# RWKV-7 stage of a bidirectional trunk: sums with the identity and with r, the diagonal blocks and a copy of U moved from VectorE to TensorE and ScalarE

## The chip, the cores and the metric

The kernel runs on one core of one Trainium2 chip. The metric is the device time of one launch in microseconds (us). The core has five engines with instruction streams of their own: TensorE (PE), VectorE (DVE), ScalarE (ACT), GpSimd (POOL) and SyncE (SP), which here issues most of the DMA transfers. TensorE's clock is granted by a throttle at one of two levels, 1.2 or 2.4 GHz; PEclk in the tables is the granted clock as a share of 2.4 GHz, averaged over a stretch.

## The reference

A trunk of two layers over 256 context and 512 latent tokens of width 1024, in fp32. Layer 0 has mLSTM heads beside differential attention, layer 1 has RWKV-7 heads beside gated linear attention, and each layer ends in an MLP. The change lies in the RWKV-7 heads alone: 8 heads of 64 channels, a scan over tokens in both directions (context first, then latents):

```python
def rwkv7_scan(r, decay, k, v, kk, a, state):
    def step(S, inp):
        r_t, w_t, k_t, v_t, kk_t, a_t = inp
        sk = jnp.einsum('bhei,bhi->bhe', S, kk_t)
        S = S * w_t[:, :, None, :] - sk[..., None] * (kk_t * a_t)[:, :, None, :] + v_t[..., None] * k_t[:, :, None, :]
        return S, jnp.einsum('bhei,bhi->bhe', S, r_t)
```

Decay, a and k come from `tanh` and `sigmoid` of small products of the tokens; kk is the unit key. After the scan the outputs are normed per head, a bonus `r . k v` is added, and a gate multiplies them. The kernel's products of this stage run on fp32 operands, for which the trace shows two records each.

## The kernel before

The scan is worked in chunks of 64 tokens. The function `rwkv` (from line 1497) takes the 8 heads as 4 pairs; a pair fills the 128 partitions, head 0 in rows 0 to 63 and head 1 in rows 64 to 127 (`OWN`; `OTH` are the other head's columns). A *unit* is four chunks of a pair in both scan directions (8 chunk matrices): per pair one unit of context and two of latents, so 12 units, u = 0 to 11. Names in a listing of the program number units from 1: `BK_8` and `AT_8` belong to u = 7.

Within a chunk the recurrence is a triangular system. With alpha the decayed unit keys (`ABD`), beta and kappa the scaled keys divided by the decay (`BK`), A = beta . alpha, and U = (I - A)^-1, state and output of a chunk are one product each with [state | values] (`X`): matrices E and F (`EF`), to which an identity (for the state) and the decayed r (`R`, for the output) are added.

`front(u)` makes what does not hang on the state:
- two products with a `tanh` behind each (L1606, tiles `th` and `ta`), +1 (L1612), the scan over the chunk (L1614), exponentials (L1633, L1634);
- `ABD` (L1640), held as a 128x128 matrix per chunk with the two heads as diagonal blocks and zeros elsewhere, in two buffers whose zeros are written once: VectorE writes head 0's blocks, GpSimd head 1's;
- `BK` (L1658 VectorE, L1660 GpSimd), `Rbd` (L1706);
- eight transposes of `ABD` on TensorE, read out by four ScalarE copies into `GT`;
- A: eight products `ABD` x `BK` (tiles `mm<-BK,abd`), read out to `AT` (L1681 ScalarE) and `GT` (L1682 VectorE);
- `DG`, the 16x16 blocks on A's diagonal: for each of four block rows a column of a 0/1 matrix (`sel`) times a slice of `AT`, summed by four VectorE instructions (L1719, L1721);
- `DG` goes by DMA to DRAM (`scrA`, L1723) and comes back with one block per partition (`lnA`, L1727). The blocks are inverted there: 14 small instructions (L1742, L1744), then L1752, a reduction on VectorE (L1754), L1755, a reduction (L1757). GpSimd does it for u from 2 on, VectorE for u = 0 and 1. The inverse goes by DMA to `scrU` (L1758).

`back(u)` fetches it (`UN`, L1766), writes it into the two halves of `U` by two masked copies (L1773), and merges blocks of 16 to 32 and 64 by small products (tiles `mg`), into `UB`.

`chain(u)` walks the four chunks: `ready` prepares `RB` and `Gt`, `solve` computes EF in PSUM and VectorE adds the identity (L1871) and R (L1874) while reading it out, `move` gives the next state (tiles `sy`, scaled into `X` at L1890) and the output (tiles `y`).

A loop over u = 0 to 14 interleaves, step by step, `chain(u-2)`, `back(u-1)`, `front(u)` and, for each pair's end, the norm of the outputs. The instructions so issued are then put in one static order per engine by a scheduler that works with modelled times; on the chip each engine executes its own list in that order and waits by semaphores. The tile `mm` in PSUM has three buffers, taken in the program's order. SP issues the transfers of the inverse in its own order, too.

Of the kernel before, what the change touches and what calls it, by code (L numbers as in the profile page):

```python
# [12 lines left out]
AF = mybir.ActivationFunctionType  # L13
ALU = mybir.AluOpType
AX = mybir.AxisListType
PSUM = bass.MemoryType.PSUM
DRAM = bass.MemoryType.DRAM
# [19 lines left out]
U_EX = 0  # L37
# [22 lines left out]
def shape_constants():  # L60
    """Constants that follow from the shapes alone: identity, block means, masks, rope tables."""
# [29 lines left out]
def shape_masks():  # L91
    """int32 masks: levels of the gated attention within blocks of 64"""
    s = np.arange(P)
    segs = {}
    a, b = s[:, None] % 64, np.arange(64)[None]
    for lv in range(6):
        m = 1 << lv
        same = (a // (2 * m)) == (b // (2 * m))
        segs[f"gf{lv}"] = same & ((a // m) % 2 == 0) & ((b // m) % 2 == 1)
        segs[f"gb{lv}"] = same & ((a // m) % 2 == 1) & ((b // m) % 2 == 0)  # L100
    segs["gd"] = a == b
    return segs
# [10 lines left out]
def layout(a):  # L113
    """tokens as columns (context, then latents); the small parameters as columns of one array"""
# [48 lines left out]
class Paced:  # L163
    """the tensor engine; instructions of side work are issued after the main work that precedes them"""
# [20 lines left out]
def trunk(ctx, tc, xc, pk, ada_w, w_in_even, w_in_odd, w_out, w_mlp_in, w_mlp_out, diff_lam, rwkv_w2, rwkv_a2,  # L185
# [40 lines left out]
    # ---------------------------------------------------------------- constants, parameters  # L226
# [84 lines left out]
    def weave(main, side, every):  # L311
        """runs main; after each `every` steps of it a step of side; then the rest of side"""
# [6 lines left out]
    def logsig(out, z, t):  # L319
        """out = log(sigmoid(z)), stable; t is scratch; out may be z only if z is SBUF"""  # L320
# [5 lines left out]
    def spread(rc, n, psum):  # L326
        """[token, tile, head] columns -> psum tiles [(h, 64), tokens] (4 tiles of 128 tokens each)"""
# [18 lines left out]
    # ---------------------------------------------------------------- adaLN modulation  # L346
# [40 lines left out]
    def norm_gain(l, which):  # L387
        """g * (1 + scale) as [P, 8, 2]"""
# [7 lines left out]
    # ---------------------------------------------------------------- building blocks  # L396
# [4 lines left out]
    def wload(pieces, kt=KT, cols=P, zero=False, rows=None):  # L401
        """pieces: (column, DRAM AP [n*128, m]) -> hi and lo parts [P, kt, cols] of all its row tiles or those in rows"""
# [21 lines left out]
    def mm3(w, at, xs, spans, bank=None):  # L424
        """three passes of one 128-column weight tile; xs: list of (hi, lo) tiles per k; yields psum per span"""
# [14 lines left out]
    def mm3_steps(w, at, xs, spans, res, group=1):  # L440
        """mm3 in steps of `group` row tiles"""
# [15 lines left out]
    def at(x, t0, t1):  # L457
        """tokens t0..t1 of a tile that holds all tokens or the latents only"""
# [31 lines left out]
    def norm_out(xT, l, which, rs, np_, spans=SPANS, first=False):  # L490
        """normed and modulated residual -> hi/lo tiles"""
# [5 lines left out]
        def shifted_parts(k):  # L497
            """adds the shift, splits"""
# [66 lines left out]
    # ---------------------------------------------------------------- scratch of the mLSTM gates  # L565
# [13 lines left out]
    # ---------------------------------------------------------------- load the residual  # L579
# [21 lines left out]
    def put_o(i, src, t0=0, t1=T, keep=None):  # L601
        """o^T tile i (fp32, SBUF) -> hi/lo parts, in DRAM or in the pool that keeps them"""
# [95 lines left out]
            # n = b - m, g = i - b, per tile: state scale exp(g + n_last), carry exp(n_last + m_prev)  # L698
# [126 lines left out]
    def head_out(i, hs, sq, sm, ps_, gain, gate):  # L825
        """rms norm of [tokens, 2 heads, 64] in natural layout, transposed, times gain (and gate) -> o^T tile i"""
# [19 lines left out]
    # ---------------------------------------------------------------- layer 0: differential attention heads  # L846
# [3 lines left out]
    def diff_prep(p, res, fin=None):  # L850
        """projections of a pair of heads, in steps"""
# [32 lines left out]
                # one Newton step on the table's result  # L884
# [65 lines left out]
    def diff_attn(fill, tail_open, tail):  # L950
        with ExitStack() as es:
# [13 lines left out]
            def scores(u):  # L965
                """softmax numerators of a unit's two maps, combined"""
# [47 lines left out]
            def finish(p, u):  # L1014
                """rms norm; the first softmax's sum divides here"""
# [28 lines left out]
            class Side:  # L1044
                """work in steps, done at a rate"""
# [55 lines left out]
    def out_proj(l, xT, oT, spans, ks=tuple(range(KT)), dts=range(KT)):  # L1101
        """adds the gated projection of the mixer tiles ks to the tiles dts of the residual"""
# [23 lines left out]
            # the first tiles' products do not wait for the sums over the residual  # L1126
# [65 lines left out]
    def tail():  # L1192
        """the part of the output projection that does not wait for the last pair of heads"""
# [33 lines left out]
    # ---------------------------------------------------------------- layer 1: gated linear attention heads, and  # L1227
    # the projections of the RWKV-7 heads
# [69 lines left out]
    def gla():  # L1298
# [4 lines left out]
        with ExitStack() as es:  # L1303
# [14 lines left out]
            # in-tile sums of the log decays  # L1318
# [69 lines left out]
                    # states: k decayed to the end of its tile  # L1388
# [640 lines left out]
```

## Time and profile before

| | |
|---|---|
| median of 3 runs | 2432.72 us (2432.2 to 2434.35) |
| span of the profiled execution, first to last instruction (no other time of that execution is given) | 2438.6 us |
| PE, DVE, ACT, POOL busy over the span | 91%, 56%, 38%, 14% |
| RWKV-7 stage, 1640 to 2005 us: PE, DVE, ACT, POOL busy | 284.5, 287.6, 182.3, 170.2 of 365 us |
| granted TensorE clock in that stage, and over the span | 0.83, 0.935 |

Before and behind that stage TensorE is busy with the large projections and the MLP. The stage is the one in which no engine is busy all the time: the table's row says 78% for PE and 79% for DVE. Busy time of PE is the union of its matmuls' times, which overlap at their ends; one record stands for a transpose.

### The profile page before, as it was taken

How to read it: one execution, taken by the hardware profiler on the slowest of the kernel's cores; microseconds unless marked ns; L12 is line 12 of the kernel's file. 1: busy time of each engine (PE TensorE's matmuls, PEld its weight loads, DVE VectorE, ACT ScalarE, POOL GpSimd, SP SyncE). 2: the span in 40 equal slices, each digit the busy share in tenths (PEclk: the TensorE clock that was granted, in tenths of full speed). 3: DMA queues.
4: the chain of work that ended last, by engine and by line, in shares of the span. 5: the costliest groups of instructions: out<-in, count | busy, mean ns of one | idle time of the engine just before them, and what ended most of it. 6: DMA issues, size and time to landing. Idle time of an engine off the chain costs nothing.

```text
span 2438.6 us, 40627 instructions
## 1 busy us (share of the span) xinstructions
PE 2219.0 (91%) x16676; PEld 1857.2 (76%) x16676; DVE 1360.4 (56%) x2616; ACT 929.7 (38%) x1785; POOL 333.5 (14%) x470
## 2 busy tenths in 40 slices
PE   5999888988899999999998999965888789999999
PEld 3888665656788888888886778854767677998997
DVE  4667645645664343343433575768778856544543
ACT  2444444545543122221323633324555543422322
POOL 3110001002100000000003021323546530000000
PEclk7999898989999999999997998976878989999999
DMA  6343468875312222222232212121010143333333
GB/s 236 78 117 103 138 191 250 257 245 169 109 54 60 61 69 62 61 61 61 67 105 58 61 44 76 64 74 23 15 31 12 32 119 91 87 96 89 94 96 95
DMA packets 293739, 232.26 MB, mean 95 GB/s; under 512 B 40705, under 2 KB 265890, under 8 KB 293554
## 3 DMA queue, kind: packets, MB, share of 16 engines
q1 hardware_dynamic: 284434, 188.65, 26.3%
q0 software_dynamic: 9120, 41.03, 5.6%
q8 instruction: 131, 2.15, 0.4%
q14 instruction: 54, 0.44, 0.1%
HBM read 203.06 MB, written 26.58 MB: 94 GB/s over the span
## 4 chain that ended last, share of the span: by engine, by line
PE 72%; DVE 11%; DMA 8%; POOL 3%; ACT 3%; issue 3%; SPq 0%; DVEq 0%; ACTq 0%; POOLq 0%
PE mm L170 60%; PE po L170 3%; PE ps L170 3%; DMA aw<-in_ada_w_dram 2%; PE gps L170 2%; DMA scrU<-lnV 1%; PE pb L170 1%; PE re L170 1%; DMA lnA<-scrA 1%; PE oy L170 1%; DMA scrA<-DG 1%; DMA UN<-scrU 1%; DMA stk<-qd 1%; POOL lnT L1742 1%; POOL lo L512 1%
## 5 line engine op out<-in xcount | busy, mean ns | idle before, releaser
L170 PE MATMUL mm<-hi,wh 128*128 128x512 f32 (+2 forms) x1816 | 495.2, 335 | 5.1 <-DVE uq L649 3.1
L398 ACT ACTIVATE wh<-wr 128x1024 fp32r<-128x1024 f32 (+1 forms) x203 | 213.7, 1052 | 750.0 <-PE mm L170 715.7
L170 PE MATMUL mm<-lo,wh 128*128 128x256 f32 (+2 forms) x1816 | 487.6, 331 | 0.4 <-DVE lo L555 0.4
L170 PE MATMUL mm<-hi,wl 128*128 128x256 f32 (+2 forms) x1816 | 485.9, 331 | 0.3 <-DVE wl L399 0.3
L170 PEld LDWEIGHTS mm<-hi,wh 128*128 128x128 f32 x1816 | 328.6, 192 | 40.5 <-issue 6.0
L170 PEld LDWEIGHTS mm<-lo,wh 128*128 128x128 f32 x1816 | 330.9, 192 | 33.5 <-issue 1.8
L170 PEld LDWEIGHTS mm<-hi,wl 128*128 128x128 f32 x1816 | 330.3, 192 | 33.0 <-issue 1.4
L399 DVE TENSOR_TENSOR wl<-wr,wh 128x1024 fp32r<-128x1024 f32 (+1 forms) x203 | 249.9, 1231 | 96.6 <-ACT wh L398 93.1
L170 PE MATMUL mm<-mhi,wl 128*128 128x512 f32 (+1 forms) x768 | 233.1, 359 | 0.5
L170 PE MATMUL mm<-mhi,wh 128*128 128x512 f32 (+1 forms) x768 | 232.6, 358 | 0.0
L170 PE MATMUL mm<-mlo,wh 128*128 128x512 f32 (+1 forms) x768 | 232.5, 358 | 0.0
L1152 DVE SCALAR_TENSOR_TENSOR xT<-mm,mod,xT 128x256 f32<-128x256 f32 (+1 forms) x96 | 60.6, 659 | 289.6 <-PE mm L170 289.6
L170 PEld LDWEIGHTS mm<-mhi,wl 128*128 128x128 f32 x768 | 144.3, 188 | 25.7 <-DVE wl L399 2.3
L170 PEld LDWEIGHTS mm<-mlo,wh 128*128 128x128 f32 x768 | 144.3, 188 | 23.3
L170 PEld LDWEIGHTS mm<-mhi,wh 128*128 128x128 f32 x768 | 144.1, 188 | 23.1
L512 POOL TENSOR_TENSOR lo<-nh,hi 128x768 fp32r<-128x768 f32 x13 | 28.8, 2240 | 695.8 <-DVE nh L507 654.6
L980 DVE TENSOR_REDUCE mx<-pb 128x1 f32<-128x768 f32 (+1 forms) x96 | 73.5, 775 | 64.8 <-PE pb L170 64.2
L1139 DVE COPY wb<-mm 128x2 f32<-128x2 f32 x64 | 10.2, 159 | 176.1 <-PE mm L170 176.1
L170 PE MATMUL mm<-aw,sv 128*32 128x256 f32 x768 | 64.6, 435 | 31.3 <-DMA aw<-in_ada_w_dram 30.9
L982 ACT ACTIVATE pp<-pb,mx 128x768 f32<-128x768 f32 (+1 forms) x96 | 72.5, 758 | 34.2 <-DVE mx L980 33.2
L399 DVE TENSOR_TENSOR mlo<-mr,mhi 128x768 fp32r<-128x768 f32 (+1 forms) x64 | 52.7, 825 | 48.3 <-ACT mhi L398 48.3
L1001 ACT ACTIVATE wT<-po 128x384 f32<-128x384 f32 (+1 forms) x80 | 37.5, 469 | 101.4 <-PE po L170 101.1
(535 smaller groups left out, 3652.5 us busy)
## 6 DMA issues: line engine op xcount, KB each, us to landing
aw<-in_ada_w_dram SPq DMA_DIRECT2D x96, 512.0 KB, 6.4
wr<-in_w_mlp_in_dram SPq DMA_DIRECT2D x64, 512.0 KB, 4.0
wr<-in_w_mlp_out_dram SPq DMA_DIRECT2D x64, 512.0 KB, 3.6
wr<-in_w_in_even_dram SPq DMA_DIRECT2D x28, 512.0 KB, 8.3
wr<-in_w_in_odd_dram SPq DMA_DIRECT2D x27, 512.0 KB, 3.8
stk<-qd POOLq DMA_DIRECT2D x32, 384.0 KB, 8.2
e<-nd SPq DMA_DIRECT2D x24, 256.0 KB, 4.2
xT<-in_xc_dram SPq DMA_DIRECT2D x8, 384.0 KB, 6.8
```

What stands on the lines that cost most here:

```text
L170: ins = getattr(self.eng, name)(*a, **k).ins
L398: act.activation(out=hi, in_=src, func=AF.Copy)
L399: dve.tensor_tensor(out=lo, in0=src, in1=hi.bitcast(F32), op=ALU.subtract)
L512: (dve if first and k in (0, 3, 6) else pool).tensor_tensor(out=lo[:, a0:a1], in0=h[:, a0:a1], in1=hi[:, a0:a1].bitcast(F32), op=ALU.subtract)
L980: dve.tensor_reduce(out=mx[:, c_:c_ + 1], in_=ps[:, :kk], axis=AX.X, op=ALU.max, negate=True)
L982: act.activation(out=pp[:, :kk], in_=ps[:, :kk], func=AF.Exp, bias=mx[:, c_:c_ + 1], accum_out=l[:, c_:c_ + 1])
L1001: act.activation(out=u["wT"][:, a0 * P:a1 * P], in_=u["po"][:, P:(1 + a1 - a0) * P], func=AF.Copy)
L1139: dve.tensor_copy(out=wb, in_=q[:, 0:nb])
L1152: dve.scalar_tensor_tensor(out=at(xT[dt], t0, t1), in0=q, scalar=mods[l][:, 5, dt, s_:s_ + 1], in1=at(xT[dt], t0, t1), op0=ALU.mult, op1=A ...
L1742: inv.tensor_tensor(out=w_, in0=A8[:, :, j, 0:j].unsqueeze(3).to_broadcast([64, 2, j, n]), in1=V8[:, :, j:j + 1, j:8].to_broadcast([64, 2, ...
```

## The change

Six pieces of `rwkv` change; the line numbers of what follows them shift by three. Comments and docstrings are dropped besides.

1. U is written by ScalarE, both halves (`U_EX`), instead of VectorE.
2. `th` + 1 is a ScalarE activation instead of a VectorE instruction.
3. `ABD` is dense, [channel, direction, chunk, 64], by two VectorE instructions over all 128 partitions; GpSimd has no part in it, and the buffer is one of a pool of two.
4. The eight transposes are 16 products of 64x64 with the identity, head 0 in the upper left quarter of TensorE's array and head 1 in the lower right, into one PSUM bank, read out by one ScalarE copy of 128x512. The products for A are 16 of 64 rows instead of eight of 128. `GT` holds alpha in columns 0 to 63 for both heads, so the copies to `Gt` reverse the halves for head 1.
5. `DG` is the sum of four products with `Dsel`, the columns of `sel` as diagonal matrices (made once), in a PSUM bank of `mm`, and one ScalarE copy.
6. EF is read out by one ScalarE copy; the identity comes in as four more products `id2` x `X` behind the four of `sy`, in the same bank, and R as four more products in `y`.

```diff
-U_EX = 0
+U_EX = 2
...
+            Dsel = tl(kp, [P, 4, P], "Dsel")
+            for e in range(4):
+                dve.tensor_scalar(out=Dsel[:, e], in0=ident, scalar1=C["sel"][:, e:e + 1], scalar2=None, op0=ALU.mult)
...
-                ABD = ABDs[u % 2]
+                ABD = tl(pp_, [P, 2, 4, 64], "abd")
...
-                dve.tensor_scalar(out=th, in0=th, scalar1=1.0, scalar2=None, op0=ALU.add)
+                act.activation(out=th, in_=th, func=AF.Copy, bias=1.0)
...
-                for h in range(2):
-                    q = OWN[h]
-                    for d in range(2):
-                        (pool if (h, d) >= (SPL_A, 0) else dve).tensor_tensor(out=ABD[q, d, :, q], in0=CH(src("kk", d))[q],
-                                                           in1=c4[q, d, :, 0:64], op=ALU.mult)
+                for d in range(2):
+                    dve.tensor_tensor(out=ABD[:, d], in0=CH(src("kk", d)), in1=c4[:, d, :, 0:64], op=ALU.mult)
...
-                for d in range(2):
-                    ps = mm()
-                    for c_ in range(4):
-                        transpose(ps[:, c_ * P:(c_ + 1) * P], ABD[:, d, c_])
-                    p3 = ps.rearrange("p (c t) -> p c t", t=P)
+                ps = mm()
+                for j in range(8):
                     for h in range(2):
-                        (dve.tensor_copy if h < GT_EV else act_copy)(GT[OWN[h], d, :, OWN[h]], p3[OWN[h], :, OWN[h]])
+                        q = OWN[h]
+                        pe.matmul(ps[q, 64 * j:64 * j + 64], ABD[q, j // 4, j % 4], ident[q, q], start=True, stop=True,
+                                  tile_position=(64 * h, 64 * h))
+                act_copy(flat(GT)[:, :, 0:64], CH(ps))
...
-                        pe.matmul(ps[:, c_ * P:(c_ + 1) * P], ABD[:, d, c_], BK[:, d, c_], start=True, stop=True)
+                        for h in range(2):
+                            q = OWN[h]
+                            pe.matmul(ps[q, c_ * P:(c_ + 1) * P], ABD[q, d, c_], BK[q, d, c_], start=True, stop=True,
+                                      tile_position=(64 * h, 64 * h))
...
-                dve.tensor_scalar(out=DG, in0=flat(AT)[:, :, 0:16], scalar1=sel(0), scalar2=None, op0=ALU.mult)
-                for e in range(1, 4):
-                    dve.scalar_tensor_tensor(out=DG, in0=flat(AT)[:, :, 16 * e:16 * e + 16], scalar=sel(e), in1=DG,
-                                             op0=ALU.mult, op1=ALU.add)
+                ps = mm()[:, 0:P]
+                for e in range(4):
+                    pe.matmul(ps.rearrange("p (j t) -> p j t", t=16), Dsel[:, e], flat(AT)[:, :, 16 * e:16 * e + 16],
+                              start=e == 0, stop=e == 3)
+                act_copy(DG.rearrange("p j t -> p (j t)"), ps)
...
-                    if more:
-                        dve.tensor_tensor(out=own(EF), in0=own(ef), op=ALU.add, in1=ident.rearrange(
-                            "p (h c) -> p h c", h=2).unsqueeze(1).to_broadcast([P, 2, 2, 64]))
-                    if lat:
-                        dve.tensor_tensor(out=oth(EF), in0=oth(ef), in1=R[:, :, c_], op=ALU.add)
+                    part = (lambda a: a) if lat and more else own if more else oth
+                    act_copy(part(EF), part(ef))
...
+                        for d in range(2):
+                            for h in range(2):
+                                pe.matmul(ps[OWN[h], 64 * d:64 * d + 64], id2[OWN[h]], X[OWN[h], d, c_, h],
+                                          start=False, stop=d == 1, tile_position=(64 * h, 64 * h))
...
+                        for own_ in range(2):
+                            for d in range(2):
...
+                                    q = OWN[h] if own_ else slice(0, P)
+                                    e = R[q, d, c_, q] if own_ else EF[:, d, 64 + 64 * h:128 + 64 * h]
```

The scheduler orders every engine's list anew. GpSimd's list at the inverse of u = 3 (its tiles end in `_4`), beside the front of u = 4 (`abd0`, `BK_5`, `kd_5`, `Rbd0`), in the kernel before:

```order
L1744 TENSOR_TENSOR lnV_4_14889<-lnV_4_14889,lnT_4_14891 64x2x3x5
L1640 TENSOR_TENSOR abd0_1_13782<-kkl_2_14552,cs_5_15077 64x4x64 x2
L1742 TENSOR_TENSOR lnT_4_14891<-lnA_4_14888,lnV_4_14889 64x24
L1744 TENSOR_TENSOR lnV_4_14889<-lnV_4_14889,lnT_4_14891 64x2x2x6
L1660 TENSOR_TENSOR BK_5_14959<-kd_5_15140,pm__5_15080 64x8x64
L1742 TENSOR_TENSOR lnT_4_14891<-lnA_4_14888,lnV_4_14889 64x14
L1660 TENSOR_TENSOR BK_5_14959<-kd_5_15140,pm__5_15080 64x8x64
L1744 TENSOR_TENSOR lnV_4_14889<-lnV_4_14889,lnT_4_14891 64x2x7
L1706 TENSOR_TENSOR Rbd0_1_13943<-rl_6_14545,cs_5_15077 64x4x64 x2
L1752 TENSOR_TENSOR lnT_4_14891<-lnA_4_14888,lnV_4_14889 64x512
L1755 TENSOR_TENSOR lnT_4_14891<-lnV_4_14889,lnW_4_14937 64x512
```

The same place in the changed kernel:

```order
L1747 TENSOR_TENSOR lnV_4_14971<-lnV_4_14971,lnT_4_14973 64x2x3x5
L1745 TENSOR_TENSOR lnT_4_14973<-lnA_4_14970,lnV_4_14971 64x24
L1747 TENSOR_TENSOR lnV_4_14971<-lnV_4_14971,lnT_4_14973 64x2x2x6
L1745 TENSOR_TENSOR lnT_4_14973<-lnA_4_14970,lnV_4_14971 64x14
L1747 TENSOR_TENSOR lnV_4_14971<-lnV_4_14971,lnT_4_14973 64x2x7
L1755 TENSOR_TENSOR lnT_4_14973<-lnA_4_14970,lnV_4_14971 64x512
L1660 TENSOR_TENSOR BK_5_15056<-kd_5_15243,pm__5_15177 64x8x64 x2
L1709 TENSOR_TENSOR Rbd0_1_13957<-rl_6_14601,cs_5_15174 64x4x64 x2
L1758 TENSOR_TENSOR lnT_4_14973<-lnV_4_14971,lnW_4_15034 64x512
```

`abd` is gone from the list, and `BK` of the next unit stands behind the first of the two large instructions instead of inside the 14 small ones.

TensorE's list around u = 7 (`BK_8`) and the merges of u = 6 (`U_7`), before:

```order
L170 MATMUL mm_402_16352<-BK_8_16119,abd1_1_13783 128x128 x4
L170 MATMUL mm_403_16372<-BK_8_16119,abd1_1_13783 128x128 x4
...
L170 MATMUL mm_405_16485<-twd_1_10820,w2_1_10804 128x256 x2
...
L170 MATMUL mg_25_16136<-U_7_16114,AT_7_15980 32x32 x32
...
L170 MATMUL mg_26_16186<-VT_13_16134,TD_13_16133 32x32 x32
...
L170 MATMUL mg_27_16248<-U_7_16114,AT_7_15980 32x32 x16
```

And in the changed kernel (`Dsel` is the selection of the diagonal blocks, `twd` the first product of u = 8's front):

```order
L170 MATMUL mg_25_16342<-U_7_16319,AT_7_16153 32x32 x32
L170 MATMUL y_7_15895<-Rbd1_1_13958,X_6_15455 64x64 x3
L170 MATMUL mm_402_16598<-BK_8_16324,abd_8_16326 64x128 x8
...
L170 MATMUL mg_27_16453<-U_7_16319,AT_7_16153 32x32 x16
...
L170 MATMUL mm_404_16664<-AT_8_16565,Dsel_1_13784 128x128 x4
...
L170 MATMUL mm_405_16729<-twd_1_10820,w2_1_10804 128x256 x2
```

A's products for the unit, and the selection of its diagonal blocks, stood ahead of the merges of the unit before (the selection on VectorE, behind the read-out of A); half of the products and the selection now stand behind the first, or the first three, steps of those merges. The selection stands behind a merge step of the unit before at eight of the eleven units that follow another (names 2, 3, 4, 6, 7, 8, 10 and 11): at 6 and 8 behind the third step, at 3 partly so, at the others behind the first. From that first step to the selection the list of these eight has 67 rows of other work in all, none at 2 and 15 at 6.

## Rows read from the trace of the kernel before

**Rows 1.** Windows: start:end, us, busy of PE, PEld, DVE, ACT, POOL; clock; DMA share

```profile
1640.00:2005.00 365.00, 284.50 (x4215) 242.47 (x4216) 287.59 (x694) 182.28 (x471) 170.17 (x265) 0.83 0.14 34
2005.00:2440.00 435.00, 426.82 (x2630) 378.43 (x2630) 209.67 (x336) 141.15 (x208) 0.00 (x0) 0.99 0.32 94
```

**Rows 2.** Instructions on tile DG: count, min/median/max ns, first to last start

```profile
L1723 SPq DMA_DIRECT2D scrA<-DG x12: 319/320/432, 1649.7 to 1964.6; - x12
```

**Rows 3.** Timeline of SP: start us, us, instruction; the transfers of DG

```profile
1734.03 0.32 SPq L1723 DMA_DIRECT2D scrA<-DG  x1
...
1761.60 0.43 SPq L1723 DMA_DIRECT2D scrA<-DG  x1
...
1783.57 0.32 SPq L1723 DMA_DIRECT2D scrA<-DG  x1
...
1825.64 0.32 SPq L1723 DMA_DIRECT2D scrA<-DG  x1
```

**Rows 4.** Chain of waits, 1738 to 1765 us, in order of time: start, us

```profile
1743.65 1.51 POOL abd L1640 x2
...
1747.50 1.34 POOL BK L1660
1748.83 0.04 issue
1748.88 2.08 PE mm L170 x8
...
1753.15 0.89 PE mm L170 x8
```

**Rows 5.** Timeline of POOL: start us, us, [idle before]; two inverses

```profile
1707.75 0.21 POOL L1742 TENSOR_TENSOR lnT<-lnA,lnV 64x14 f32<-64x14 f32 x1 [4.47 <-DMA lnA<-scrA]
...
1713.50 2.17 POOL L1752 TENSOR_TENSOR lnT<-lnA,lnV 64x512 f32<-64x512 f32 x1
...
1739.37 0.21 POOL L1742 TENSOR_TENSOR lnT<-lnA,lnV 64x14 f32<-64x14 f32 x1 [3.90 <-DMA lnA<-scrA]
...
1750.60 2.18 POOL L1752 TENSOR_TENSOR lnT<-lnA,lnV 64x512 f32<-64x512 f32 x1
```

**Rows 6.** Timeline of DVE: the reads of U

```profile
1789.47 0.48 DVE L1773 TENSOR_SCALAR U<-UN,cs 128x128 f32<-128x128 f32 x2 [2.24 <-DMA UN<-scrU]
...
1987.00 0.48 DVE L1773 TENSOR_SCALAR U<-UN,cs 128x128 f32<-128x128 f32 x2 [5.98 <-DMA UN<-scrU]
```

**Rows 7.** Timeline of PE, 1987 to 2003 us: merges and a late chunk

```profile
1987.63 1.06 PE L170 MATMUL mg<-U,AT 32*32 32x32 f32 x64 [2.85 <-DVE U L1773]
...
1994.04 0.69 PE L170 MATMUL mg<-U,AT 32*32 32x32 f32 x32
...
2001.41 0.45 PE L170 MATMUL sy<-X,EF 128*64 128x64 f32 x8
2001.69 0.40 PE L170 MATMUL y<-EF,X 128*64 128x64 f32 x8
2002.03 0.71 PE L170 MATMUL re<-RB,Gt 128*128 128x128 f32 x4
```

**Rows 8.** ACT by line and form, stage: busy us, mean ns | idle before

```profile
L1825 ACT ACTIVATE GT<-mm 64x256 f32<-64x256 f32 x48 | 18.2, 378 | 27.8 <-PE mm L170 27.2
L1825 ACT ACTIVATE RB<-re 128x256 f32<-128x256 f32 x43 | 16.4, 382 | 23.3 <-PE re L170 22.2 <-ACT Gt L1825 0.7
...
L1912 ACT ACTIVATE yo<-y 128x512 f32<-128x512 f32 x3 | 1.8, 597 | 0.1
```

**Rows 9.** DVE by line and form, stage: what the change takes away

```profile
L1871 DVE TENSOR_TENSOR EF<-re,cs 128x256 f32<-128x256 f32 x42 | 17.7, 421 | 11.9 <-PE re L170 11.0
...
L1721 DVE SCALAR_TENSOR_TENSOR DG<-AT,cs,DG 128x128 f32<-128x128 f32 x36 | 12.3, 342 | 0.4
L1874 DVE TENSOR_TENSOR EF<-re,Rbd 128x256 f32<-128x256 f32 x29 | 12.0, 414 | 2.1 <-PE re L170 2.0
...
L1612 DVE TENSOR_SCALAR th<-th 128x512 f32<-128x512 f32 x11 | 6.1, 558 | 6.2 <-ACT th L1606 6.2
L1773 DVE TENSOR_SCALAR U<-UN,cs 128x128 f32<-128x128 f32 x24 | 6.1, 297 | 22.0 <-DMA UN<-scrU 22.0
...
L1719 DVE TENSOR_SCALAR DG<-AT,cs 128x128 f32<-128x128 f32 x12 | 4.4, 363 | 0.4
```

More of the change, by code (lines that the diff above doesn't have):

```diff
@@ L1543, in rwkv @@
             dve.memset(CH(rst)[:, :, 0:1], 0.0)
-            ABDs = zeros(tz, [P, 2, 4, P], "abd")
             load_constants(kp, 2)
+            Dsel = tl(kp, [P, 4, P], "Dsel")
+            for e in range(4):
+                dve.tensor_scalar(out=Dsel[:, e], in0=ident, scalar1=C["sel"][:, e:e + 1], scalar2=None, op0=ALU.mult)
             UBs = zeros(kp, [P, 2, 4, P], "UB", 1, dve)
@@ L1681, in front @@
                         act.activation(out=AT[q, d], in_=p3[q, :, q], func=AF.Copy)
-                        dve.tensor_tensor(out=GT[q, d, :, o_], in0=p3[q, :, o_], op=ALU.mult,
+                        dve.tensor_tensor(out=GT[q, d, :, 64:128], in0=p3[q, :, o_], op=ALU.mult,
                                           in1=C["mlt"][q].unsqueeze(1).to_broadcast([64, 4, 64]))
@@ L1716, in front @@
                 sA, sU = scrA[u % 3], scrU[u % 3]
-                sel = lambda n: C["sel"][:, n:n + 1]
                 DG = tl(pp_, [P, 8, 16], "DG")
-                dve.tensor_scalar(out=DG, in0=flat(AT)[:, :, 0:16], scalar1=sel(0), scalar2=None, op0=ALU.mult)
-                for e in range(1, 4):
-                    dve.scalar_tensor_tensor(out=DG, in0=flat(AT)[:, :, 16 * e:16 * e + 16], scalar=sel(e), in1=DG,
-                                             op0=ALU.mult, op1=ALU.add)
+                ps = mm()[:, 0:P]
[3 more added lines that the diff above has]
+                act_copy(DG.rearrange("p j t -> p (j t)"), ps)
                 sp.dma_start(out=sA, in_=DG.rearrange("p j t -> p (j t)"))
@@ L1856, in ready @@
                         pe.matmul(ps[:, d * P:d * P + P], UB[:, d, c_], GT[:, d, c_], start=True, stop=True)
+                    half_ = lambda a: a.rearrange("p d (a c) -> p d a c", a=2)
                     for h in range(2):
-                        (dve.tensor_copy if h < G_EV else act_copy)(Gt[c_ % 2][OWN[h], h], D2(ps[OWN[h], 0:256]))
+                        o_ = half_(Gt[c_ % 2][OWN[h], h])
+                        act_copy(o_[:, :, ::-1] if h else o_, half_(D2(ps[OWN[h], 0:256])))
                     yield
@@ L1884, in move @@
                                 pe.matmul(ps[OWN[h], 64 * d:64 * d + 64], EF[:, d, 192 * h:192 * h + 64], X[:, d, c_, h],
-                                          start=True, stop=True, tile_position=(0, 64 * h))
+                                          start=d == 0, stop=False, tile_position=(0, 64 * h))
+                        for d in range(2):
+                            for h in range(2):
+                                pe.matmul(ps[OWN[h], 64 * d:64 * d + 64], id2[OWN[h]], X[OWN[h], d, c_, h],
+                                          start=False, stop=d == 1, tile_position=(64 * h, 64 * h))
                         sy = ps[:, 0:128].rearrange("p (d c) -> p d c", d=2)
@@ L1892, in move @@
                     if lat:
-                        for d in range(2):
-                            j = 4 * (g - 1) + c_
-                            j = j if d == 0 else 7 - j
-                            for h in range(2):
-                                e = EF[:, d, 64 + 64 * h:128 + 64 * h]
-                                pe.matmul(S["y"][OWN[h], 64 * j:64 * j + 64], X[:, d, c_, h], e if d == 0 else e[:, ::-1],
-                                          start=(g == 1 and c_ == 0 and d == 0), stop=(g == 2 and c_ == 3 and d == 1),
-                                          tile_position=(0, 64 * h))
+                        for own_ in range(2):
+                            for d in range(2):
+                                j = 4 * (g - 1) + c_
+                                j = j if d == 0 else 7 - j
+                                for h in range(2):
+                                    q = OWN[h] if own_ else slice(0, P)
+                                    e = R[q, d, c_, q] if own_ else EF[:, d, 64 + 64 * h:128 + 64 * h]
+                                    pe.matmul(S["y"][OWN[h], 64 * j:64 * j + 64], X[q, d, c_, h],
+                                              e if d == 0 else e[:, ::-1],
+                                              start=(g == 1 and c_ == 0 and d == 0 and not own_),
+                                              stop=(g == 2 and c_ == 3 and d == 1 and own_ == 1),
+                                              tile_position=(64 * h if own_ else 0, 64 * h))
                     yield
```

## The prediction, made before the changed kernel was run

> **What bounds the kernel now.** I read the windows first. The change lies in the stretch from 1640 to 2005 us, and there no engine is full: of 365 us PE is busy 284.5, DVE 287.6, ACT 182.3 and POOL 170.2, at a granted clock of 0.83, that is part of the time at the lower of the two levels; behind it PE has 426.8 of 435 at 0.99 [rows 1]. So what is saved on an engine is not saved on the clock; the stage is set by waits that go in a circle, and I looked for the circle's pace. The transfers of `DG` give it: 12 of them from 1649.7 to 1964.6 us, 314.9 us for 11 steps, 28.6 us each [rows 2]. The steps are uneven: 27.6 us from the first to the second of those shown, then 22.0, then 42.1 [rows 3].
>
> Then I asked what lies inside a step. The chain of waits shows the front of unit u = 4: POOL `abd`, POOL `BK`, and only then PE's products for A; a group of eight passes took 2.08 us behind that wait, and 0.89 a little later [rows 4]. So PE is found at half speed after idling. POOL's timeline says why the front waits: the 14 small steps of an inverse took 5.8 us where nothing stood between (1707.75 to 1713.50) and 11.2 us where `abd`, `BK` and `Rbd` did (1739.37 to 1750.60) [rows 5]. Both suffer: the inverse comes 5.5 us later, and the front waits for an engine that is busy with the inverse. Last, the way from `DG`'s transfer to the read of `U`, with three more transfers and the inverse in it: 27.9 us for the transfer at 1761.60 (read at 1789.47), and 22.4 us for the last unit (1964.6 to 1987.00), with no front left on POOL [rows 2, 3, 6].
>
> **What each part costs.** *VectorE* loses the rows of `EF` (17.7 and 12.0), `DG` (4.4 and 12.3), `th` (6.1) and `U` (6.1), 58.6 us together [rows 9]. It keeps `ABD`, as two instructions over 128 partitions instead of two over 64. DVE is no full engine, so these 58.6 us count only where an instruction is waited for.
>
> *ScalarE* loses 48 `GT` copies of 378 ns, 18.2 us. It gets, priced by 597 ns for a 128x512 read-out and 382 ns for a 128x256 one [rows 8], 12 `GT` copies (7.2), 28 full and 16 half `EF` copies (22.8), 12 `th` (7.2), 24 `U` and 12 `DG` (at most 13.8): net about +33, to 215 of 365. I cost that at nothing as work; its cover is ScalarE's idle time, most of which ends with a product of PE [rows 8]. As a queue it is a rival below.
>
> *TensorE.* `id2` and R add 76 groups of four tiled products. Late in the stage, at full speed, one `sy` group took 0.28 us start to start and `y` 0.34 [rows 7]. I take 0.35 for a group set between others: 27 us. `Dsel` adds 12 times eight passes, 0.89 each [rows 4]: 10.7 us. The transposes and A's products stream as many columns as before, two tiles side by side, with perhaps 0.3 us more per unit: 4 us. Together about 42 us at full clock and up to 84 at half, against 80.5 us of PE's idle time. I put it at nothing while other waits last, and at its price in the tail: from the read of the last `U` on PE has hardly a gap, with 0.62 us for the pair `sy`, `y` [rows 7]. Five chunks there times 0.71 us for the two groups, with a little for the longer `EF` copy, is +4 us (bounds 0 and 8).
>
> The two groups run in another tiling than their neighbours. By the row, the 0.62 us for 16 half-width passes, two side by side, is more than their columns alone. The Trainium skill ("TensorEngine Tiling (Array Packing)", "Key Properties") says that changing the tiling mode, not just the tile, drains TensorE. If that did not hold here, the same rows without a gap would put a group at 0.22 us (eight passes of half the columns, two side by side: a quarter of the 0.89 us for eight), and the tail at +2; with it, +4.
>
> *GpSimd* loses `abd`; in its new order `BK` and `Rbd` stand, with few exceptions, behind the inverse's small steps. What I need from this is the way from `DG` to `U`. Its least seen value is 22.4 us, its value with a loaded POOL 27.9 [rows 2, 3, 6]. I take 22.4, because what made the difference of 5.5 us is in size just what stood inside that inverse [rows 5], and most of it leaves. VectorE's two inverses I treat alike.
>
> *The order.* In eight of eleven units the selection now stands behind the merges of the unit before. There the step becomes a closed loop: `DG` to `U`, `U` to the first merge, to the selection, to the next `DG`. The second half: 0.63 us from `U` to the merge (1987.00 to 1987.63), 1.06 for the merge [rows 6, 7], 0.89 for `Dsel` [rows 4], 0.38 for the copy [rows 8]: 3.0 us, eight times 24. Between lie 67 rows of PE's order, at 0.31 us a row (0.62 for two [rows 7]): 20.8 us. The bounds of this term are 24, where all of these have run while PE waited for `U`, and 66, where they run at half clock. The first half is 8 x 22.4 = 179.2, and 2.7 for one `BK` (two of 1.34 [rows 4]) and 1.3 for one `Rbd` that still stand inside an inverse: 183. Three units keep the selection ahead of the merges; between 22.0 and 27.6 [rows 3] I give them the middle, 24.8 each: 74.4.
>
> Sum: 183 + 44.8 + 74.4 = 302.3 us for eleven steps, against 314.9: -12.6. With the tail, -8.6. The front of the first unit I leave as it is (half a microsecond less for `abd` in front of it; the selection's 1.3 us by PE and ACT stands for 1.4 by DVE). From the span of 2438.6 us this gives 2430.0. The span is 5.9 us above the median of the runs; taking that off, **2424 us**. Its own range is 2408 to 2440: the second half of the loop between 24 and 66 us, and the way to `U` half a microsecond either way per unit.
>
> **Rivals.**
>
> *The loop is closed but not short (slower).* That the selection stands behind the merges is sure; that the way from `DG` to `U` falls to 22.4 us is not. Against it: the rows `U` on DVE ended 22.0 us of waiting for the transfer of `UN` in ten cases [rows 9]. The same wait now stands in ScalarE's list, with `Gt`, `A`'s and `EF`'s copies behind it and all of PE behind these; the chain's `EF` was on another engine before. A copy stuck there holds the chain, which by the static order holds the front. Each microsecond more costs eight. At the middle of the two measured ways, 25.2 us, the kernel takes 2424 + 8 x 2.8 = **2446 us**; at 27.9 it is 2468. It decides from 24.1 us on: there the gain of 13.6 us up to the bound of slower is used up. For it speaks that the only step of 22.4 us seen had no other unit's front beside it; against it, that GpSimd is rid of its longest foreign work.
>
> *VectorE sets the pace (faster).* DVE has 287.6 of 365 us, the largest share [rows 1], and its rows show little waiting beside their work: 0.4 us before `DG`'s 36 instructions [rows 9]. If the instructions stand in line there all the way, the 58.6 us come off in full: 2438.6 - 58.6 + 4 - 5.9 = **2378 us**. Against it: the 22.0 us before `U` and 11.0 before `EF` are waits for others, and 77 us of idle time are too much for an engine that sets the pace.
>
> *No change.* The pace stays at 28.6 us because PE takes over: what it gains from shorter waits it spends on 42 us of new passes, or more at the lower clock. Then only the tail is left: 2438.6 + 4 - 5.9 = **2437 us**. For it speaks that PE's 284.5 and 42 are 327 of 365, more than any engine has now; against it, that PE's busy time includes passes at half clock [rows 4], which a fuller PE would run faster.
>
> **How the numbers follow.** I give my forecast 0.42, the closed loop that stays long 0.27, no change 0.15, VectorE's pace 0.13, and 0.03 to something not thought of. What a measurement of this kernel can tell from no change is 0.2%, 4.9 us: faster is below 2427.9, slower above 2437.6. Of the forecast's own range two thirds lie below, a quarter between, the rest above: 0.28, 0.10, 0.04. No change splits around 2437 into 0.10 within and 0.05 above; the unknown goes two to one to the fast side. So faster is 0.28 + 0.13 + 0.02 = 0.43, within 0.2% is 0.10 + 0.10 = 0.20, and slower 0.27 + 0.04 + 0.05 + 0.01 = 0.37. The range that holds 8 in 10 reaches from 2390 (most of the way to VectorE's case) to 2452 (the long loop at 26 us).
>
> **What would show it.** In the new trace the steps between `DG`'s transfers should average 27.5 us, with 22 to 24 us from a transfer to the read of `U`, and POOL's small steps back at 6 us; PE's busy time should rise by 25 to 45 us, DVE's fall by 55 to 62. The forecast is wrong if the way to `U` stays near 25 us or more, if ScalarE waits for `UN` with products of the chain idle behind it, or if steps fall well below 25 us, which the closed loop forbids.

## The result: 3% slower, outside the range

The changed kernel takes 2509.3 us (2504.3 to 2513.3, 4 runs) beside 2433.5 us, a ratio of 1.0306 (1.0288 to 1.0323). I had forecast 2424 us and a range that ended at 2452. The profiled executions have spans of 2438.6 and 2502.4 us; they lie closer together than the medians, since that of the kernel before was longer than its median and that of the changed kernel the shortest of its four. The loss lies in the RWKV-7 stage alone. Its window (the columns are those of [rows 1]), and the transfers of `DG` (those of [rows 2]), in the changed kernel:

```profile
1640.00:2075.00 435.00, 349.87 (x5420) 295.17 (x5421) 241.58 (x538) 208.65 (x531) 155.05 (x242) 0.83 0.14 35
```

```profile
L1726 SPq DMA_DIRECT2D scrA<-DG x12: 319/322/326, 1643.6 to 2018.9; - x12
```

Over the whole execution PE is busy 59 us longer (25 to 45 had been forecast) and VectorE 48 us shorter (55 to 62 had been forecast), first before, then changed:

```profile
PE 2219.0 (91%) x16676; PEld 1857.2 (76%) x16676; DVE 1360.4 (56%) x2616; ACT 929.7 (38%) x1785; POOL 333.5 (14%) x470
PE 2278.0 (91%) x17860; PEld 1903.8 (76%) x17860; DVE 1312.4 (52%) x2460; ACT 954.9 (38%) x1845; POOL 315.2 (13%) x444
```

The step from `DG` to `DG` rose from 28.6 us to 375.3 / 11 = 34.1. From the first instruction to the first transfer the kernel is 6.1 us quicker, the 11 steps are 60.5 us longer, and what follows the last transfer is 9.5 us longer: the 63.8 us between the spans.

The inside of a step, as means over the first eleven units, from start to start in the two traces unless said otherwise:

| us | before | changed |
|---|---|---|
| the 14 small steps of the inverse | 9.3 | 7.6 |
| from the end of L1758 (L1755 before) to the second reduction on VectorE | 2.0 | 2.7 |
| transfer of `DG` to the read of `U` | 27.8 | 26.9 |
| read of `U` to the next transfer of `DG` | 0.8 | 7.3 |

One step of the changed kernel, from the timelines of SP, POOL, DVE and ACT (columns as in [rows 5]):

```profile
1914.22 0.33 SPq L1726 DMA_DIRECT2D scrA<-DG  x1
...
1953.60 0.32 SPq L1726 DMA_DIRECT2D scrA<-DG  x1
```

```profile
1924.86 2.17 POOL L1755 TENSOR_TENSOR lnT<-lnA,lnV 64x512 f32<-64x512 f32 x1
1930.19 1.67 POOL L1758 TENSOR_TENSOR lnT<-lnV,lnW 64x512 f32<-64x512 f32 x1 [3.17 <-DVE lnW L1757]
```

```profile
1933.92 2.84 DVE L1641 TENSOR_TENSOR abd<-kkc,cs 128x256 f32<-128x256 f32 x2
1936.68 0.41 DVE L1854 TENSOR_TENSOR RB<-re,cs 128x256 f32<-128x256 f32 x1
1937.02 0.67 DVE L1760 TENSOR_REDUCE lnV<-lnT 64x64 f32<-64x512 f32 x1
```

```profile
1942.64 0.69 ACT L1774 ACTIVATE U<-UN,cs 128x128 f32<-128x128 f32 x2 [2.60 <-DMA UN<-scrU]
```

The small steps are free of `abd`, as forecast; then POOL waits for the first reduction, and the second comes late on VectorE behind `abd`, whose two instructions took 2.84 us there. 28.4 us pass from the transfer to `U`, and 11.0 more to the next transfer.

### The profile page after: what moved, and what is told of

The parts are those of the page before. It is cut to its first block, busy times and chain, and to the rows that moved or that the text cites. A ratio compares the mean times of both kernels' runs of the same rounds, so it can differ in the third digit from the quotient of the medians.

```text
span 2502.4 us, 42854 instructions
## 1 busy us (share of the span) xinstructions
PE 2278.0 (91%) x17860; PEld 1903.8 (76%) x17860; DVE 1312.4 (52%) x2460; ACT 954.9 (38%) x1845; POOL 315.2 (13%) x444
## 4 chain that ended last, share of the span: by engine, by line
PE 72%; DVE 9%; DMA 8%; issue 4%; ACT 4%; POOL 3%; SPq 0%; POOLq 0%; ACTq 0%; DVEq 0%
PE mm L170 59%; PE po L170 3%; PE ps L170 3%; DMA aw<-in_ada_w_dram 2%; PE re L170 2%; DMA lnA<-scrA 1%; PE gps L170 1%; DMA stk<-qd 1%; PE pb L170 1%; PE y L170 1%; DMA scrU<-lnV 1%; POOL lnT L1745 1%; POOL lnV L1747 1%; PE sy L170 1%; DMA scrA<-DG 1%
## 5 line engine op out<-in xcount | busy, mean ns | idle before, releaser
L1139 DVE COPY wb<-mm 128x2 f32<-128x2 f32 x64 | 10.2, 159 | 177.6 <-PE mm L170 177.6
L170 PE MATMUL re<-RB,Gt 128*128 128x128 f32 (+1 forms) x384 | 69.3, 320 | 12.6 <-ACT Gt L1828 8.7
```

Source lines behind the costliest of these rows:

```text
L170: ins = getattr(self.eng, name)(*a, **k).ins
L1139: dve.tensor_copy(out=wb, in_=q[:, 0:nb])
```

## Experiments

**One part undone.** From the changed kernel, each time one part was put back (the lines are those of the diff above): EF with its products, DG, U, or the dense keys.

```diff
# un_EF
-                    act_copy(part(EF), part(ef))
+                        dve.tensor_tensor(out=oth(EF), in0=oth(ef), in1=R[:, :, c_], op=ALU.add)
...
# un_DG
-                act_copy(DG.rearrange("p j t -> p (j t)"), ps)
+                    dve.scalar_tensor_tensor(out=DG, in0=flat(AT)[:, :, 16 * e:16 * e + 16], scalar=sel(e), in1=DG,
+                                             op0=ALU.mult, op1=ALU.add)
# un_U
-U_EX = 2
+U_EX = 0
# un_ABD
-                ABD = tl(pp_, [P, 2, 4, 64], "abd")
+                ABD = ABDs[u % 2]
```

> The changed kernel (2509 us) with EF read out by VectorE again, identity and R added there, and without the products id2 x X and R in y. Theory A (closed loop): the loss is the time from the read of U to the next transfer of DG, 7.3 us a step against 0.8 before, and it comes from the selection of DG standing behind the merges; that stays, so 2490 to 2505 us, with the steps still 32 us or more. Theory B (added passes): PE is busy 350 us in the stage against 285, 65 us more, and these products are the largest part of it; without them 2455 us or less. Theory C (ScalarE in order): EF's copies stand behind the read of U, which waits 26.4 us for its transfer; without EF on ScalarE the chain is free of it, 2450 us or less, with the wait for UN unchanged.

> The changed kernel (2509 us) with DG's selection by four VectorE instructions again, no Dsel products and no bank of PSUM for them. Theory A (closed loop through the selection): the way from U to the next transfer of DG falls from 7.3 to about 1 us in the mean, the step from 34.1 to about 28, so about 2440 us. Theories B and C (added passes of PE, ScalarE in order): Dsel is 11 us of PE and 12 copies of 0.28 us, so 2495 us or more.

> The changed kernel (2509 us) with U written by VectorE again. Theory C (ScalarE in order): the 26.4 us of waits for UN leave ScalarE, and copies behind it run earlier, so 2480 us or less. Theories A and B: the selection stays behind the merges and PE's passes stay, within 10 us of 2509.

> The changed kernel (2509 us) with ABD as 128x128 blocks by VectorE and GpSimd, eight whole transposes, four copies to GT and eight whole products for A. Theory A: the loop stays closed, and abd is back inside the inverse's small steps (7.6 us in the mean against 9.3 before): 2505 to 2530 us. Theory B: 4 us at most: within 10 us of 2509. A fourth one, D (VectorE serves the front first, and the inverse's reductions wait behind the large abd instructions, 2.7 us a step): 2480 to 2495 us.

Measured: 2481.9 us, 2480.7, 2507.6 and 2509.2, with ratios to before of 1.0191 (1.0158 to 1.0225), 1.0184 (1.0155 to 1.0213), 1.0292 and 1.0302. EF and DG give back 27 and 29 us, U and the dense keys nothing. That fitted none of the theories: A had asked for 4 to 19 us from EF and 70 from DG, B for 54 or more from EF and at most 14 from DG, C for 29 or more from U, and D (in the text on `un_ABD`) for 14 to 29 from the dense keys. Taking the wait for `UN` off ScalarE gained nothing, so there is no sign that it is a cause.

**Passes, copies, and the selection's place.** `zero_passes` adds the products alone to the kernel before, `no_id` takes them alone from the changed one (it leaves the identity and R out of the sums), `front_first` holds `Dsel` ahead of the first merge, `on_EF` makes EF's part alone. In `front_first` the front is also issued ahead of the merges and at another pace (`WF`), so its lists differ from those of the changed kernel in more than the selection's place.

```diff
# zero_passes (kernel before)
+                                pe.matmul(ps[OWN[h], 64 * d:64 * d + 64], Zt[OWN[h]], X[OWN[h], d, c_, h],
+                                          start=False, stop=d == 1, tile_position=(64 * h, 64 * h))
# front_first (changed kernel); the edge at each product of the first merge
-WF = 1
+WF = 99
...
+                            tc.add_manual_dep(pe.last, nx["dsel"].name, mybir.DependencyInfo(
+                                mybir.DependencyClass.NoSync, mybir.DependencyReason.DATA), reason="paced")
```

> The kernel before (2435 us), its VectorE work as it is, with the 76 groups of four tiled products added in sy and y, against a tile of zeros, so nothing is summed twice. Theory B (added passes of PE set the loss): the changed kernel without these groups and with EF on VectorE had 34 us less of busy PE and was 27 us faster, so here 25 to 40 us slower, 2460 to 2475 us. Theory A (loop closed by the selection) and C (EF's copies in ScalarE's order): PE has 80 us of idle time in the stage, so within 10 us of 2435.

> The changed kernel (2509 us) without the products id2 x X and R in y, but with EF still copied by ScalarE: the identity and R are left out of the computation. Theory B: as much faster as with EF on VectorE, 2475 to 2485 us. Theory C (EF's copies in ScalarE's order): nothing is gained by it, 2500 to 2510 us.

> The changed kernel with one more rule for TensorE's order: the first merge of a unit stands behind the selection of the next unit's diagonal blocks, at all units (in the changed kernel it stands ahead at eight). No work is added or taken away. Theory A: the step, 34.1 us, falls to 28 to 31, so 2440 to 2475 us. Theory B: the same passes in another order, within 15 us of 2509.

> The kernel before with one part of the change: EF by one ScalarE copy, identity and R as products. Theory B: 25 to 40 us slower, 2460 to 2475 us, as with the products against zeros. If the loss needs the whole change (an order that only all parts together bring about): 2425 to 2440 us.

Measured: 2489.6 us (1.0231, 1.0201 to 1.0261), 2482.4 (1.0212), 2506.5 (1.0305) and 2456.7 (1.0101, 1.0078 to 1.0125). `front_first` speaks against theory A, and with it against my picture of the stage: with the selection ahead of all merges nothing is gained.

```profile
L1727 SPq DMA_DIRECT2D scrA<-DG x12: 319/322/328, 1642.5 to 2025.9; - x12
```

Its steps are 34.9 us; the way from `DG` to `U` fell to 24.6 us, and that from `U` to the next `DG` rose to 10.2, though no merge stands ahead of the selection there. Since its lists are new elsewhere too, it does not give the price of the selection's place alone. `no_id` looks like theory B, `zero_passes` too, but overshoots; `on_EF` lies between its two expected ranges. PE's timeline of `zero_passes` shows what a group costs:

```profile
1918.13 0.45 PE L170 MATMUL sy<-X,EF 128*64 128x64 f32 x8
1918.51 0.45 PE L170 MATMUL sy<-X,Zt 64*64 64x64 f32 x8
1918.89 0.45 PE L170 MATMUL y<-EF,X 128*64 128x64 f32 x8
1919.27 0.45 PE L170 MATMUL y<-Zt,X 64*64 64x64 f32 x8
```

0.38 us from start to start (granted clock 1.00), so 29 us for 76 groups, on an engine with 80 us to spare. They cost 56.

**Other parts alone, on the kernel before.** DG, the dense keys, `th` + 1, and the last two with U.

> The kernel before (2434 us) with one part of the change: DG's selection by four products with Dsel and a ScalarE copy. Theory B (PE's stream, at about one to two us per us of added passes): 12 us of passes, 2446 to 2458 us. Theory E (the parts cost only together): within 8 us of 2434. If the selection's way through two more queues costs 2 us a step: 2455 to 2465 us.

> The kernel before with one part of the change: dense ABD by VectorE, 16 tiled transposes and one copy, A by 16 half products. Theory B: 4 to 6 us of passes, 2437 to 2446 us. Theory F (the half products of A start early, at the first operand, and end late; from BK to A's read-out a step takes 3 to 4 us longer wherever they are): 2465 to 2480 us. If the freed GpSimd counts, 2410 to 2430 us.

> The kernel before with one part of the change: th + 1 by ScalarE. No passes are added, and VectorE loses 6 us; the scheduler still orders every engine anew. Theory B: within 5 us of 2434. Theory G (any new order is worse than the one of before, whatever the work): 15 us slower or more.

> The kernel before with dense ABD and tiled products, th + 1 and U on ScalarE; EF and DG as before, so hardly any added passes. If the parts add (the changed kernel lost 27 us of its 75 by EF's products and 28 by DG's): 2450 to 2460 us. Theory B alone: 2435 to 2445 us. Theory F: 2465 to 2480 us.

Measured: 2483.6 us (1.0200, 1.0179 to 1.0220), 2479.6 (1.0186, 1.0171 to 1.0201), 2437.3 (1.0009, 0.9996 to 1.0023) and 2458.7 (1.0100, 1.0083 to 1.0118). DG, the dense keys and EF cost 49, 45 and 23 us alone, and all parts together 76. Dense keys with `th` and U cost less than dense keys. `on_DG` is above all that was expected of it; theory F's range holds for the dense keys alone and fails with `th` and U. Sizes that add up so badly are hardly those of work. What all dear kernels share is that the scheduler ordered every engine's list anew. But it did so in `on_TH` too, which cost nothing: by the order of starts in the stage, 65% of PE's instructions that it shares with the kernel before and 71% of VectorE's stand at another place than there (87% and 82% in `zero_passes`), by 19 places in the mean on PE (51 in `zero_passes`). Theory G as first put, that any new order is worse, had asked for 15 us or more there and is wrong; what is left of it is that some orders are.

**Work and order apart.** So I held the order: at the stage's end an edge without a semaphore is laid from each instruction to the next of its engine, in the order in which a given other kernel has them (`HOLD` is that list); the added products stand right behind their `sy` or `y`, and the other instructions that the other kernel lacks are left to the scheduler.

```diff
+            names = {i.name: i for i in nc.cur_bb.bb.instructions}
+            for steps in HOLD.values():
+                n = steps[0]
+                for step in steps[1:]:
+                    tc.add_manual_dep(names[f"I-{n + step}"], f"I-{n}", mybir.DependencyInfo(
+                        mybir.DependencyClass.NoSync, mybir.DependencyReason.DATA), reason="hold")
+                    n += step
```

> The kernel before (2435 us), instruction for instruction, but each engine's list in the RWKV-7 stage is held in the order that the scheduler chose for the kernel with the products against zeros (2490 us). Theory B (added passes cost the time): no pass is added, 2425 to 2445 us. Theory G (the new order costs it): 2470 to 2490 us.

> The kernel with the 76 groups of products against zeros (2490 us in its own order), held in the order of the kernel before, each group right behind its sy or y. Theory B: the passes are all there, 2475 to 2495 us. Theory G: 2437 to 2455 us, the price of the passes on the chain and in the tail alone (76 groups of 0.38 us are 29 us at most).

> The changed kernel (2509 us) with all instructions that it shares with the kernel before held in the order of before; the new ones (Dsel, the copies of DG, GT, EF and U, th + 1, abd) are placed by the scheduler, the id2 and R products right behind sy and y. Theory B: all its work is there, 2490 to 2515 us. Theory G: 2425 to 2460 us.

> The kernel before with EF's part alone (2457 us in its own order), held in the order of before where instructions are shared. Theory G: 2425 to 2445 us, since VectorE loses 30 us and PE gets 29 us of passes. Theory B: 2450 to 2465 us.

> The changed kernel with EF on VectorE and without the id2 and R products, held in the order of before where instructions are shared. Theory G with EF as the costly part of the work: 2435 to 2447 us (2461 less about 20). If the dense keys, the selection and U on ScalarE cost the 27 us: 2455 to 2465 us.

> The kernel before with dense abd and tiled products, th + 1 and U on ScalarE (2459 us in its own order), held in the order of before where instructions are shared. GpSimd loses 19 us and VectorE 12, and hardly a pass is added: theory G says 2415 to 2435 us; if it is 2450 or more, the dense keys cost by their work.

| run | us | ratio to before (interval) |
|---|---|---|
| work_before_order_zero | 2478.3 | 1.0180 (1.0158 to 1.0203) |
| zero_order_before | 2443.4 | 1.0051 (1.0028 to 1.0074) |
| after_order_before | 2460.7 | 1.0109 (1.0084 to 1.0135) |
| on_EF_order_before | 2455.0 | 1.0074 (1.0048 to 1.0100) |
| after_less_EF_order_before | 2442.2 | 1.0039 (1.0023 to 1.0054) |
| ABD_TH_U_order_before | 2430.5 | 0.9989 (0.9974 to 1.0005) |

The first row settles that an order alone can cost this much. The kernel before, not an instruction more or less, takes 45 us longer in another order. One such order was tried; that of the changed kernel was not laid on the old work. The second is its mirror: with the 29 us of passes the kernel costs 10 us more in the old order (12 by the ratio) and 56 in its own. In the last row such edges and three parts of the change together cost nothing that can be told, so the edges by themselves are not dear. One row went against theory G: `on_EF_order_before` was to come down to 2425 to 2445 us and stayed at 2455.0, 22 us above before, where its own order had 23. So what EF's part costs alone is its work more than its order, as far as the noise lets one tell. The transfers of `DG`, first of the old work in the new order, then of the products against zeros in the old order:

```profile
L1861 SPq DMA_DIRECT2D scrA<-DG x12: 319/326/662, 1642.6 to 1996.9; - x12
```

```profile
L1875 SPq DMA_DIRECT2D scrA<-DG x12: 319/320/432, 1653.8 to 1968.3; - x12
```

Steps of 32.2 and of 28.6 us. In the old order the passes cost the steps nothing. From the start of the last transfer that execution takes 483.8 us instead of 474.0, 9.8 more; it is one execution, 10 us above its kernel's median. In the other order `DG` to `U` fell to 26.6 us and `U` to the next `DG` rose from 0.8 to 5.6: as in the changed kernel (7.3), the next unit's front comes late behind `U`.

What the order does can be read at u = 7. POOL and PE in the kernel before:

```profile
1837.00 1.03 POOL L1640 TENSOR_TENSOR abd<-kkl,cs 64x256 f32<-64x256 f32 x1
...
1838.72 0.90 POOL L1640 TENSOR_TENSOR abd<-kkl,cs 64x256 f32<-64x256 f32 x1
1839.70 2.60 POOL L1660 TENSOR_TENSOR BK<-kd,pm__8_16240 64x512 f32<-64x512 f32 x2
1842.38 2.18 POOL L1752 TENSOR_TENSOR lnT<-lnA,lnV 64x512 f32<-64x512 f32 x1
```

```profile
1839.68 1.11 PE L170 MATMUL mm<-cs,abd 128*128 128x128 f32 x4 [0.49 <-POOL abd L1640]
1840.59 1.91 PE L170 MATMUL re<-RB,Gt 128*128 128x128 f32 x8
...
1843.57 2.32 PE L170 MATMUL mm<-BK,abd 128*128 128x128 f32 x16
```

And the same instructions in `work_before_order_zero`:

```profile
1838.57 2.17 POOL L1890 TENSOR_TENSOR lnT<-lnA,lnV 64x512 f32<-64x512 f32 x1
1840.70 2.69 POOL L1798 TENSOR_TENSOR BK<-kd,pm__8_16240 64x512 f32<-64x512 f32 x2
1843.36 1.68 POOL L1778 TENSOR_TENSOR abd<-kkl,cs 64x256 f32<-64x256 f32 x2
```

```profile
1844.27 1.93 PE L170 MATMUL mm<-cs,abd 128*128 128x128 f32 x8 [3.28 <-POOL abd L1778]
...
1846.65 0.70 PE L170 MATMUL sy<-X,EF 128*64 128x64 f32 x8 [0.44 <-DVE EF L2009]
1847.13 0.64 PE L170 MATMUL y<-EF,X 128*64 128x64 f32 x8
1847.70 2.08 PE L170 MATMUL re<-RB,Gt 128*128 128x128 f32 x8
1849.57 0.63 PE L170 MATMUL re<-cs,BK 128*128 128x128 f32 x2
1849.99 1.06 PE L170 MATMUL re<-Rbd,BK 128*128 128x128 f32 x4
1850.85 2.31 PE L170 MATMUL mm<-BK,abd 128*128 128x128 f32 x16
```

In the good order `abd` is made inside the small steps of the inverse, and PE's transposes are done before `BK` is ready at 1842.3; A follows at 1843.57, behind a few of the chain's products. In the other, POOL finishes the inverse's large instruction first; PE stops 3.28 us for `abd`, the chain's products that stand behind the transposes wait with it, and A, whose `BK` is ready at 1843.4, starts 7.5 us later, behind them. From `BK` to A it is 1.0 us in the mean over the units from the second on before, and 2.9 in the other order. That this one place stands for the whole is my reading, and it is not shown: u = 7 is one of the two units with the longest way from `BK` to A; 1.9 us is about half of what a step grew by; and in the changed kernel POOL makes no `abd`, so there it must be other places. The sum of the waits was not taken apart edge by edge. Nor is the clock parted from the waits: over the stage, from the first scan to the last EF, the same instructions keep PE busy 20 us longer in the other order, at a lower mean clock (the last rows of this document).

## Why the prediction was wrong

Two terms of the sum for the steps failed, "GpSimd" and "The order". In the prediction's own division of the eleven steps, with what the changed kernel's trace has for each:

| us | forecast | measured |
|---|---|---|
| the eight units, `DG` to `U` | 183 | 214.8 |
| the eight units, `U` to the next `DG` | 44.8 (24 to 66) | 73.1 |
| the three other units, whole steps | 74.4 | 87.5 |

The first line is the step "GpSimd": the way from `DG` to `U` was taken at 22.4 us and fell from 27.8 to 26.9 only, so the gain did not come; a way near 25 us or more was the prediction's own sign of being wrong. The second line is the step "The order", and all that a step lost against before lies there: from `U` to the next `DG` it went from 0.8 to 7.3 us. I read the new lists and saw that the selection had moved behind the merges, but priced the move as 67 rows of 0.31 us in one loop. In `front_first`, where the selection is ahead of them, the step was no shorter (34.9 us). The order held shows what the new lists cost: of the 76 us, 48.5 go when the changed kernel runs in the old order (2509.3 to 2460.7). The rest, in that order, by differences of medians: EF's part 18.6 (2460.7 to 2442.2), DG's selection 11.6 (to 2430.5), dense keys, `th` and U nothing that can be told from before. By the ratios the first two are 17 and 12 us, uncertain by some 7 and 5. In the traces 11.0 us of EF's part lie behind the last transfer and 5.5 in the steps; all of DG's lies in the steps.

The terms, one by one:
- *GpSimd.* The small steps did fall, from 9.3 to 7.6 us, but the way from `DG` to `U` stayed at 26.9 us where I took 22.4: about 50 us over eleven steps. [Rows 5] showed one inverse with 11.2 us; over the first eleven units' nine that GpSimd makes it was 8.8 before and is 6.6 now, and 0.7 us are lost again before the second reduction. The last unit's 22.4 us was no value to be had in the middle: in the changed kernel it is 20.2 us there and 25.0 to 28.4 in all others. [Rows 5] also showed `abd` and `BK` inside an inverse, and I took this for two works in each other's way. The 1837 us rows above show what they did there: feed the next front while the inverse was under way. In the old order the way is 28 us with and without POOL's `abd` (27.8, and 27.7 in `ABD_TH_U_order_before`), and the step is 28.6 and 28.0.
- *VectorE.* Its busy time fell by 48 us, less than forecast, and bought nothing; the rival that gave 2378 us is dead.
- *TensorE.* 0.38 us for a group where I took 0.35. Late rows of the kernel before had 0.28 for `sy` [rows 7]; among neighbours in another tiling it is 0.38, both at a granted clock of 1.00, for columns that by the prediction's estimate need 0.22. The trace agrees with the Trainium skill there ("TensorEngine Tiling (Array Packing)", "Key Properties": a change of the tiling mode drains the engine), as far as such differences can show it. The `sy` in front of an added group takes 0.38 us instead of 0.28 as well, so a group there costs up to 0.48. I had put the passes at nothing in the steps and at +4 us in the tail. In the old order that holds: nothing in the steps, 9.8 us in the tail, over my bound of 8 (in the changed kernel 9.5).
- *ScalarE and the selection.* Both cost at nothing; in the old order EF's part costs 18.6 us, of which the passes explain 10, and DG's 11.6. Of EF's rest, 9 us, I know only that it comes with the read-out's move from VectorE to ScalarE; this was not tested further.
- *The rivals.* The slower one had the sign, and its condition came true: at 26.9 us for the way to `U` its price is 2424 + 8 x 4.5 = 2460 us, 49 short of the measured time. Its reason, a ScalarE list held up by `UN`, is not borne out by `un_U`. A rival that the new list is worse by itself was missing, though I had shown the lists.

Theory B in its first form, that the passes set the loss, was wrong as well: it explained `no_id` and `zero_passes` by the work, and the order held took four fifths of the latter away.

## What to carry to other kernels

Where a scheduler fixes every engine's list, the list is a term of the sum: here 45 us for the same instructions, more than any part of the work in the old order. Not every new list is dear (`on_TH`), and not every dear part is dear by its list (EF). Before a part is judged by putting it in or taking it out, hold the order of the good kernel and let only the new instructions move; a part that is dear in its own order may be free in the other (dense keys, `th` and U: 2459 and 2431 us). And a foreign instruction inside a chain of an engine that works in order may be what feeds the next unit in time.

## What was not expected of the hardware

In `zero_order_before`, with 76 added groups (29 us by 0.38 us each) and PE busy rising from 76% to 82% of the stage (from the first scan to the last EF, by the union of its matmuls), the step kept its 28.6 us: at this share, PE had room. The granted clock differed with the order, not only with the work. Over that same stage, for the same instructions, its mean is 0.82 before and 0.78 in the other order, with PE busy 291 of 383 and 311 of 420 us (first before, then `work_before_order_zero`; columns as in [rows 1]):

```profile
1629.07:2012.06 382.99, 291.02 (x4288) 248.40 (x4288) 301.95 (x726) 186.95 (x481) 175.70 (x272) 0.82 0.16 38
1622.60:2042.10 419.50, 310.95 (x4293) 266.20 (x4294) 308.74 (x727) 186.91 (x482) 178.00 (x272) 0.78 0.14 35
```

How much of the 45 us is this clock and how much the waits that came with it is open.
